# Branch B of a hybrid encoder: four query heads of a key group in one product, meta products behind wide value products, one output tile for two pairs

## The chip, the cores and the metric

The kernel runs on one core of a Trainium2 chip, in one launch. The metric is the device time of one execution in microseconds (us); the median of three runs before the change is 1885.11 us (1883.92 to 1886.2). Five engines run side by side on a core: TensorE (PE; its weight loads are shown as PEld), VectorE (DVE), ScalarE (ACT), GpSimd (POOL) and SyncE (SP), which issues nearly all DMAs here. TensorE writes into PSUM banks, from which ScalarE and VectorE copy results into SBUF.

## The reference

One layer of an encoder is applied to two request groups with shared weights: a prompt of 2048 tokens and a sample of 512, each with 16 meta tokens in front, model width 1024. All is in float32. After a norm, one input projection gives queries, keys, values and gates for two attention branches, whose outputs are projected, gated, merged and projected again. Branch A is attention over a token grid. Branch B, which this case is about, is windowed attention with 8 query heads and 2 key and value heads of width 64, so each key group serves four query heads:

```python
s_band = jnp.einsum('bnqkgd,bnckd->bnkgqc', qr, k_band).astype(f32) * scale + band_bias
s_band = jnp.where(visible[:, None, None], s_band, NEG_INF)
s_meta = jnp.einsum('bnqkgd,bmkd->bnkgqm', qr, km).astype(f32) * scale + meta_bias
p = jax.nn.softmax(jnp.concatenate([s_band, s_meta, sink_col], axis=-1), axis=-1).astype(v.dtype)
o_real = (jnp.einsum('bnkgqc,bnckd->bnqkgd', p[..., :C], v_band)
          + jnp.einsum('bnkgqm,bmkd->bnqkgd', p[..., C:C + N_META], vm))
```

A block of 128 queries sees its own block of keys and the ones before and behind it (three blocks, or two at the ends of a sequence), the 16 meta keys, and a sink logit that counts in the denominator alone.

## The kernel before

Tokens are cut into five windows of 512 (window 0 is the sample). The input projections come first, up to about 980 us. Then follows the attention with the output side of the layer filled in between. Numbers are kept as a high and a low part in a reduced float32 (F32R), so that a product of two such numbers is made of two or three matmuls: high by high, high by low, low by high.

**Units and their order.** `units` (L1508) lists for each window 32 units of branch A (`unit_a`, L1074) and 16 of branch B (`unit_b`, L1171). A unit of branch B is a key group `gh` (two), a query block `n` (four) and a pair of heads `i` (two): 128 queries by two heads. Each unit is a generator with stages: loads (L1181 to L1205), scores (L1207 to L1227), normalisation (L1228), transposes and eviction (L1232), products with the values (L1264). The main loop (L1563) advances the units in a software pipeline: in step i it runs the loads of unit i+4, the scores of i+2, the normalisation of i+1, some dense work, the transposes of unit i, dense work again, and the products of unit i-1 last. The dense work (`fill`, L1544) is the output side of the layer, in portions of six matmuls of 512 columns; a unit of branch B gets one portion in each of its two places, or a little less in window 0. The order on TensorE is as written; on VectorE, ScalarE, GpSimd and SP a scheduler orders instructions.

**A unit of branch B.** Per head, two matmuls (L1223, L1224) give the scores of 128 queries against 402 columns (16 meta keys, the sink, a pad column, three blocks of 128) or 274 (two blocks). VectorE adds the bias and finds the maximum (L1047), ScalarE takes the exponential with its sum (L1054). The two heads lie in one tile `prs`, the first with its meta columns last and the second with its meta columns first (L1212), so that the meta columns of both heads are neighbours; for this, key and bias tiles hold the meta columns a second time behind the blocks (L1191, L1204, L1215). VectorE normalises one head and ScalarE the other (L1229).

TensorE then transposes each key block of each head (L1243) and once the 32 meta columns of the two heads (L1246). ScalarE copies the high part into `ph_` (L1250), VectorE the low part into `pl_` (L1251). These two tiles have 14 places of 128 columns; units use the places from 0 and from 6 in turn. For the meta columns, three copies (L1260 to L1262) fill one of two tiles `pms`: high part, low part, and the high part again, 96 rows in all.

The products: for each key block, one of the high probabilities (256 columns, two heads) with the values' high and low part side by side (128 weight columns, L1267) and one of the low probabilities with the high part (64 weight columns, L1272). Before the last low one stand two products of 128 columns, one per head, of `pms` with `vms`, the meta values laid out for the three parts and 64 weight columns (L1270). The sum's upper half holds the low values' part; ScalarE copies it (L1274) and VectorE adds the halves into `y32` (L1277), 128 columns a head. After the last block, `y32` is multiplied by the gate (L1280) and split into high and low (`y_split`, L1067): multiplication and low part on GpSimd, the copy on ScalarE. For the very last group VectorE does GpSimd's part. Each `y32` is 512 columns of two heads; the tag has two buffers, which branch A uses too (L1110).

**What else is on the engines.** Portions of dense work bring weight casts (L207 on ScalarE, L208 on GpSimd), gate multiplications, squares and sums. In branch A, L1141 are the transposes, L1156 and L1158 the products, L1164 the sum. `dense_fin` (L1361) uses the transposes' PSUM banks for L170 and L185.

Of the kernel before, what the change touches and what calls it, by code (L numbers as in the profile page):

```python
# [17 lines left out]
P = 128  # L18
# [77 lines left out]
def encoder_block(ctx: ExitStack, tc: tile.TileContext, xT, x_end, w_in, w_pa, w_pb, w_o, norm_g, final_g,  # L96
# [945 lines left out]
    HALF = 416  # L1042
# [24 lines left out]
    def y_split(br, w, p, y32, eng=nc.gpsimd):  # L1067
        if p == 0:
            ys[br, w] = tuple(yp.tile([P, 4, WTOK], F32R, tag=f"y{br}{i}", name=f"y{br}{i}{w}") for i in range(2))
        yh, yl = ys[br, w]  # L1070
        nc.scalar.copy(yh[:, p, :], y32)
        eng.tensor_sub(yl[:, p, :], y32, f32(yh[:, p, :]))

    def unit_a(w, p, h, g, sh):  # L1074
# [34 lines left out]
        if g == 0 and h == 0:  # L1109
            sh["y"] = at.tile([P, WTOK], F32, tag="y32", name="y32")  # L1110
# [14 lines left out]
        pr = at.tile([P, 2 * HALF], F32, tag="pr", name="pr", bufs=3)[:, :WTOK]  # L1125
# [45 lines left out]
    def unit_b(w, gh, n, i, sh):  # L1171
# [12 lines left out]
        if n == 0 and i == 0:  # L1184
            q = sh["q"] = ld.tile([P, 2, 2, WTOK], F32R, tag="q", name="q")
            for j in range(2):
                move(q[:, j], qb_d[w, p + j].rearrange("(h d) i t -> (d i) h t", h=2))
            bt = sh["b"] = ld.tile([P, 2, 2, EXTRA + 3 * P + N_META], F32, tag="ba", name="bb")
            for j in range(2):
                move(bt[:, j, :, : EXTRA + 3 * P], bias_b[p + j])  # L1190
                move(bt[:, j, 0, EXTRA + 3 * P :], bias_b[p + j][:, 0, :N_META])  # L1191
        if n == 0 and first:
            bt0 = sh["b0", i] = ld.tile([P, 2, EXTRA + 2 * P + N_META], F32, tag="b0", name="bb0")
            move(bt0[:, :, : EXTRA + 2 * P], bias_b0[p])
            move(bt0[:, 0, EXTRA + 2 * P :], bias_b0[p][:, 0, :N_META])
# [3 lines left out]
        if i == 0:  # L1199
            kt = sh["k"] = ld.tile([P, 2, EXTRA + 3 * P + N_META], F32R, tag="kd", name="kbt")  # L1200
            move(kt[:, :, EXTRA : EXTRA + nbk * P],
                 kb_d[gs].rearrange("d j i t -> (d j) i t")[:, :, b0 : b0 + nbk * P])
            move(kt[:, :, :EXTRA], kbm_d[gs].rearrange("d j i t -> (d j) i t"))
            move(kt[:, :, ncol : ncol + N_META], kbm_d[gs].rearrange("d j i t -> (d j) i t")[:, :, :N_META])  # L1204
        kt, q, z = sh["k"], sh["q"][:, i], sh.get(("z", i))  # L1205
        yield
        if n == 0:  # L1207
            sh["y", i] = at.tile([P, WTOK], F32, tag="y32", name="y32")
        y32 = sh["y", i]
        bt = sh["b0", i] if first else sh["b"][:, i]  # L1210
        prs = at.tile([P, 2 * HALF], F32, tag="pr", name="prs", bufs=3)
        cols = slice(HALF - ncol, HALF), slice(HALF, HALF + ncol)  # L1212
        k0 = HALF - ncol + EXTRA - N_META, HALF + EXTRA
        if nbk == 2 and not first:
            nc.vector.tensor_copy(bt[:, 0, ncol : ncol + N_META], bt[:, 0, :N_META])  # L1215
        sm = sums_of()
        for h in range(2):
# [4 lines left out]
            ks = slice(N_META * (1 - h), N_META * (1 - h) + ncol)  # L1222
            nc.tensor.matmul(s[:, :ncol], q[:, h, qs], kt[:, 0, ks], start=True, stop=False)  # L1223
            nc.tensor.matmul(s[:, :ncol], q[:, h, qs], kt[:, 1, ks], start=False, stop=True)  # L1224
            nm = scores_max(s, ncol, bt[:, h, ks])
            exps(prs[:, cols[h]], s[:, :ncol], nm, sm[:, h : h + 1])
        yield  # L1227
        rd = inverse(sm)  # L1228
        for h in range(2):  # L1229
            normalise(prs[:, cols[h]], prs[:, cols[h]], rd[:, h : h + 1], on_act=h == 1)  # L1230
        yield
        slots = [("k", j) for j in range(nbk)] + [("m", 0)]  # L1232
        parts = []
        c0 = 6 * ((2 * n + i) % 2)
        for half in range(0, len(slots), 2):
            tp = ps_p.tile([P, WTOK], F32, tag="tp", name="tp")
            part = slots[half : half + 2]
            nk = sum(1 for t, _ in part if t == "k")
            for m, (t, j) in enumerate(part):
                c = 2 * m * P  # L1240
                if t == "k":
                    for h in range(2):
                        nc.tensor.transpose(tp[:, c + h * P : c + (h + 1) * P],  # L1243
                                            prs[:, k0[h] + j * P : k0[h] + (j + 1) * P], ident)
                else:
                    nc.tensor.transpose(tp[: 2 * N_META, c : c + P], prs[:, HALF - N_META : HALF + N_META], ident)  # L1246
            if nk:
                x = slice(c0 + 2 * half, c0 + 2 * half + 2 * nk)
                tb = tp[:, : nk * 2 * P].rearrange("p (b t) -> p b t", t=P)
                nc.scalar.copy(ph_[:, x], tb)  # L1250
                nc.vector.tensor_sub(pl_[:, x], tb, f32(ph_[:, x]))  # L1251
            for m, (t, j) in enumerate(part):
                c = slice(2 * m * P, 2 * (m + 1) * P)
                if t == "k":
                    x = slice(c0 + 2 * (half + m), c0 + 2 * (half + m) + 2)
                    parts.append((j, *(t[:, x].rearrange("p b t -> p (b t)") for t in (ph_, pl_))))
                else:
                    pm = pms[(2 * n + i) % 2]
                    tm = tp[:32, c.start : c.start + P]
                    nc.scalar.copy(pm[0:32], tm)  # L1260
                    nc.vector.tensor_sub(pm[32:64], tm, f32(pm[0:32]))
                    nc.scalar.copy(pm[64:96], f32(pm[0:32]))  # L1262
        yield
        o = ps_o.tile([P, WTOK], F32, tag="o", name="ob")  # L1264
        for m, (j, hi, lo) in enumerate(parts):
            vb = sh["v"][:, (b0 - tlo) // P + j, :]
            nc.tensor.matmul(o[:, : 2 * P], vb, hi, start=(m == 0), stop=False, skip_group_check=True)  # L1267
            if m == nbk - 1:
                for h in range(2):
                    nc.tensor.matmul(o[:64, h * P : (h + 1) * P], vms[:, gh, h, :], pms[(2 * n + i) % 2], start=False,  # L1270
                                     stop=False, skip_group_check=True)
            nc.tensor.matmul(o[:64, : 2 * P], vb[:, :64], lo, start=False, stop=m == nbk - 1, skip_group_check=True)  # L1272
        ol = at.tile([64, WTOK], F32, tag="ol", name="ol", bufs=1)[:, : 2 * P]
        nc.scalar.copy(ol, o[64:128, : 2 * P])  # L1274
        for h in range(2):
            hs = slice(64 * h, 64 * h + 64)
            nc.vector.tensor_add(y32[hs, qs], o[:64, h * P : (h + 1) * P], ol[:, h * P : (h + 1) * P])  # L1277
        if n == 3:
            eng = nc.vector if w == NWIN - 1 and gh else nc.gpsimd
            eng.tensor_mul(y32, y32, z)  # L1280
            y_split("b", w, p, y32, eng)
# [253 lines left out]
    pms = [yp.tile([96, P], F32R, tag=f"pms{i}", name=f"pms{i}") for i in range(2)]  # L1535
    vms = yp.tile([96, 2, 2, 64], F32R, tag="vms", name="vms")
# [3 lines left out]
    with tc.manual_schedule(engines={E.PE}):  # L1540
# [17 lines left out]
        vbm = vbm_d.rearrange("m g (h f) -> m g h f", h=2)  # L1558
        for h in range(2):
            for r, part in ((0, 0), (32, 0), (64, 1)):  # L1560
                move(vms[r + 16 * h : r + 16 * h + 16, :, h], vbm[:, :, part, :])
        next(units[0][2])
        for i in range(N):  # L1563
# [12 lines left out]
            fill(share)  # L1576
            next(units[i][2])
# [3 lines left out]
            if i:  # L1581
# [111 lines left out]
```

## Time and profile before

| | |
|---|---|
| median of 3 runs | 1885.11 us |
| the profiled execution | 1884.6 us, its span 1882.6 us |
| branch B's units | from 1072.5 us (first transposes) to 1802 us (last products), beside branch A's |
| 1390 to 1472 us, branch B of window 2: TensorE busy | 81.74 of 82 us |
| the same: ScalarE, VectorE, GpSimd | 71.62, 65.54, 43.38 us |

The span runs from the program's first instruction to its last in one profiled execution. A group line of the profile has line, engine, operation, tiles (out<-in), shape and count, then busy time and the mean of one in ns, then the engine's idle time before and what ended it. A line of the order of time has start, duration, engine, line, operation, tiles and shape, with "xN" for N merged instructions, and in brackets idle time before it. Matmuls are pipelined: a matmul's duration holds its latency, and the distance from one start to the next tells what it takes of TensorE's time.

### The profile page before, as it was taken

How to read it: one execution, taken by the hardware profiler on the slowest of the kernel's cores; microseconds unless marked ns; L12 is line 12 of the kernel's file. 1: busy time of each engine (PE TensorE's matmuls, PEld its weight loads, DVE VectorE, ACT ScalarE, POOL GpSimd, SP SyncE). 2: the span in 40 equal slices, each digit the busy share in tenths (PEclk: the TensorE clock that was granted, in tenths of full speed). 3: DMA queues.
4: the chain of work that ended last, by engine and by line, in shares of the span. 5: the costliest groups of instructions: out<-in, count | busy, mean ns of one | idle time of the engine just before them, and what ended most of it. 6: DMA issues, size and time to landing. Idle time of an engine off the chain costs nothing. (4 is left out here: it accounts for less than half of the span.)

```text
span 1882.6 us, 29816 instructions
## 1 busy us (share of the span) xinstructions
PE 1857.5 (99%) x9797; PEld 1585.1 (84%) x9797; DVE 1326.1 (70%) x2961; ACT 1144.5 (61%) x2528; POOL 729.2 (39%) x558
## 2 busy tenths in 40 slices
PE   8999999999999999999999999999999999999998
PEld 6988888888888888888888888888888888888887
DVE  8985667556477565544457888878887877888874
ACT  6444444434365444444456797797789778878932
POOL 2005343323203222322324435656744763685420
PEclk9999999999999999999999999999999999999999
DMA  7675666655295677644259878977986997697483
GB/s 262 199 195 183 194 184 182 209 188 179 84 341 185 189 216 199 208 139 160 104 187 316 274 221 265 305 213 249 319 275 187 316 307 227 218 315 259 118 301 133
DMA packets 288145, 414.35 MB, mean 220 GB/s; under 512 B 117736, under 2 KB 162360, under 8 KB 286456
## 3 DMA queue, kind: packets, MB, share of 16 engines
q1 hardware_dynamic: 287704, 412.45, 68.1%
q8 instruction: 78, 1.28, 0.3%
q14 instruction: 75, 0.61, 0.1%
q10 hardware_dynamic: 288, 0.01, 0.0%
HBM read 303.46 MB, written 108.91 MB: 219 GB/s over the span
## 5 line engine op out<-in xcount | busy, mean ns | idle before, releaser
L208 POOL TENSOR_TENSOR wt<-wraw,wt 128x512 fp32r<-128x512 f32 x164 | 213.0, 1317 | 266.9 <-ACT wt L207 266.8
L850 PE MATMUL pa<-u,wt 128*128 128x512 f32 x1008 | 244.5, 392 | 2.1 <-ACT wt L207 1.1
L850 PE MATMUL pa<-u,x 128*128 128x512 f32 x984 | 236.7, 389 | 0.4 <-ACT u L861 0.4
L850 PEld LDWEIGHTS pa<-u,wt 128*128 128x128 f32 x1008 | 189.9, 189 | 42.4 <-ACT wt L207 1.5
L207 ACT CAST wt<-wraw 128x512 fp32r<-128x512 f32 x312 | 178.0, 619 | 74.8 <-PE mm L148 29.8
L850 PEld LDWEIGHTS pa<-u,x 128*128 128x128 f32 x984 | 184.5, 188 | 39.2 <-ACT u L861 0.8
L821 POOL TENSOR_TENSOR s<-wraw,raw 128x512 f32<-128x512 f32 x40 | 58.2, 1456 | 279.4 <-DVE x L208 279.4
L146 PE MATMUL mm<-u,wt 128*128 128x512 f32 (+2 forms) x416 | 150.4, 362 | 7.1 <-ACT u L334 7.1
L816 POOL TENSOR_TENSOR s<-raw 128x512 f32<-128x512 f32 x40 | 58.1, 1454 | 232.8 <-DMA raw<-in_w_in_dram 116.0
L147 PE MATMUL mm<-u,wt 128*128 128x512 f32 (+2 forms) x416 | 146.8, 353 | 1.1 <-DVE u L335 1.1
L148 PE MATMUL mm<-u,wt 128*128 128x512 f32 (+2 forms) x416 | 146.6, 352 | 0.0
L208 DVE TENSOR_TENSOR wt<-wraw,wt 128x512 fp32r<-128x512 f32 x148 | 104.5, 744 | 52.3 <-ACT wt L207 52.1
L850 PE MATMUL pe<-u,wt 128*128 128x512 f32 x504 | 121.4, 390 | 0.0
L850 PE MATMUL pc<-u,wt 128*128 128x512 f32 x504 | 121.1, 389 | 0.0
L850 PE MATMUL pe<-u,x 128*128 128x512 f32 x480 | 115.3, 389 | 0.0
L850 PEld LDWEIGHTS pe<-u,wt 128*128 128x128 f32 x504 | 94.6, 188 | 19.6
L850 PEld LDWEIGHTS pc<-u,wt 128*128 128x128 f32 x504 | 94.6, 188 | 19.6
L1145 DVE TENSOR_TENSOR pl<-tp,ph 128x384 fp32r<-128x384 f32 (+6 forms) x160 | 94.9, 593 | 20.9 <-ACT ph L1144 18.7
L1144 ACT CAST ph<-tp 128x384 fp32r<-128x384 f32 (+6 forms) x160 | 81.5, 510 | 43.0 <-PE tp L1141 41.4
L146 PE MATMUL pso<-mh,wt 128*128 128x512 f32 x256 | 107.1, 418 | 0.0
L829 POOL TENSOR_TENSOR s<-wraw,s 128x512 f32<-128x512 f32 x40 | 54.0, 1350 | 136.3 <-DVE wt L208 136.3
L850 PEld LDWEIGHTS pe<-u,x 128*128 128x128 f32 x480 | 90.1, 188 | 18.7
(258 smaller groups left out, 5024.8 us busy)
## 6 DMA issues: line engine op xcount, KB each, us to landing
wraw<-in_w_in_dram SPq DMA_DIRECT2D x86, 512.0 KB
raw<-in_w_in_dram SPq DMA_DIRECT2D x40, 512.0 KB
q<-qa SPq DMA_DIRECT2D x40, 512.0 KB
wraw<-in_w_o_dram SPq DMA_DIRECT2D x32, 512.0 KB
kbt<-kb SPq DMA_DIRECT2D x32, 384.0 KB
qa<-evq SPq DMA_DIRECT2D x20, 512.0 KB
qb<-evq SPq DMA_DIRECT2D x20, 512.0 KB
ka<-evk SPq DMA_DIRECT2D x20, 512.0 KB
```

The source lines that it names most:

```text
L146: nc.tensor.matmul(ps, wh, uh, start=first, stop=False)
L147: nc.tensor.matmul(ps, wh, ul, start=False, stop=False)
L148: nc.tensor.matmul(ps, wl, uh, start=False, stop=last)
L207: nc.scalar.copy(h, r)
L208: low[0] = (eng or lo_eng[0]).tensor_sub(l, r, f32(h)).ins
L816: eng.tensor_add(s1, a21, a22)
L821: eng.tensor_sub(s3, a11, a21)
L829: eng.tensor_sub(s4, a12, s2)
L850: nc.tensor.matmul(ps, wt[:, a, s], u[:, b, kk, :], start=first and kk == 0 and i == 0, stop=kk == 3 and i == 2, skip_group_check=True)
L1144: nc.scalar.copy(ph_[:kb, a], tb)
L1145: nc.vector.tensor_sub(pl_[:kb, a], tb, f32(ph_[:kb, a]))
```

## The change

The two units of a block (`i` = 0 and 1) now share what comes after the transposes, so that four heads go through the products together.

- `ph_` and `pl_` hold a key block as four places, one a head; the two units fill two each. The products of a pair run once, in the second unit's last stage: high and low of 512 columns per key block. The first unit's last stage is empty.
- GpSimd multiplies the meta columns of each unit by the inverse sums into a small tile `mt` (four heads of 16 columns). One transpose for the pair, behind the second unit's last key block, gives 64 rows; ScalarE copies the high part into rows 0 to 63 of `pms`, VectorE the low part into rows 64 to 127. There is one `pms`. `vms` has 128 weight columns per head, and four meta products a pair: one behind each high product, the rest behind the first low product.
- The copy of the sum's upper half is 512 wide, and two additions of 256 columns (two pairs of heads by 128) go into an output tile for two pairs, which has one buffer. Branch A's head pairs share this tile two by two as well.
- The meta columns stay first (in a window's first block of a sequence, last), with no second copy of them; normalisation covers the key blocks alone. The bias of a sequence's first block lies behind the other in one tile: the tile `b0`, the extra DMAs and the copy of L1215 go.
- In the main loop, products of unit i-1 come before the transposes of unit i wherever one of the two is of branch B.

```diff
@@ unit_a @@
         if g == 0 and h == 0:
-            sh["y"] = at.tile([P, WTOK], F32, tag="y32", name="y32")
+            if p % 2 == 0:
+                pair[0] = at.tile([P, 2, WTOK], F32, tag="y32", name="y32", bufs=1)
+            sh["y"] = pair[0][:, p % 2]
@@ unit_b @@
         for h in range(2):
-            normalise(prs[:, cols[h]], prs[:, cols[h]], rd[:, h : h + 1], on_act=h == 1)
+            normalise(prs[:, h, band], prs[:, h, band], rd[:, h : h + 1], on_act=h == 1)
+        nc.gpsimd.tensor_mul(mt[:, 2 * i : 2 * i + 2, :], prs[:, :, meta : meta + N_META],
+                             rd[:, :, None].broadcast_to([P, 2, N_META]))
         yield
...
+            end = i == 1 and j0 + 2 > nbk
+            if end:
+                tm = tp[: 4 * N_META, 2 * nk * P : (2 * nk + 1) * P]
+                nc.tensor.transpose(tm, mt.rearrange("p n m -> p (n m)"), ident)
             if nk:
-                x = slice(c0 + 2 * half, c0 + 2 * half + 2 * nk)
...
+                ph, pl = (t[:, 4 * j0 : 4 * (j0 + nk)].rearrange("p (j i h) t -> p j i h t", i=2, h=2)[:, :, i]
+                          for t in (ph_, pl_))
+                tb = tp[:, : nk * 2 * P].rearrange("p (j h t) -> p j h t", h=2, t=P)
+                nc.scalar.copy(ph, tb)
+                nc.vector.tensor_sub(pl, tb, f32(ph))
+            if end:
+                nc.scalar.copy(pms[:64], tm)
+                nc.vector.tensor_sub(pms[64:], tm, f32(pms[:64]))
+        yield
+        if i == 0:
+            yield
+            return
         o = ps_o.tile([P, WTOK], F32, tag="o", name="ob")
-        for m, (j, hi, lo) in enumerate(parts):
+        for j in range(nbk):
             vb = sh["v"][:, (b0 - tlo) // P + j, :]
-            nc.tensor.matmul(o[:, : 2 * P], vb, hi, start=(m == 0), stop=False, skip_group_check=True)
-            if m == nbk - 1:
-                for h in range(2):
-                    nc.tensor.matmul(o[:64, h * P : (h + 1) * P], vms[:, gh, h, :], pms[(2 * n + i) % 2], start=False,
+            hi, lo = (t[:, 4 * j : 4 * j + 4].rearrange("p b t -> p (b t)") for t in (ph_, pl_))
+            for y, (out, vals, src) in enumerate(((o, vb, hi), (o[:64], vb[:, :64], lo))):
+                nc.tensor.matmul(out, vals, src, start=j + y == 0, stop=j + y == nbk, skip_group_check=True)
+                for m in (range(nbk, 4) if j == 0 else ()) if y else (j,):
+                    nc.tensor.matmul(o[:, m * P : (m + 1) * P], vms[:, gh, m, :], pms, start=False,
                                      stop=False, skip_group_check=True)
-            nc.tensor.matmul(o[:64, : 2 * P], vb[:, :64], lo, start=False, stop=m == nbk - 1, skip_group_check=True)
-        ol = at.tile([64, WTOK], F32, tag="ol", name="ol", bufs=1)[:, : 2 * P]
-        nc.scalar.copy(ol, o[64:128, : 2 * P])
+        ol = at.tile([64, WTOK], F32, tag="ol", name="ol", bufs=1)
+        nc.scalar.copy(ol, o[64:128])
+        ov, lv = (t.rearrange("p (i h t) -> p i h t", i=2, h=2) for t in (o[:64], ol))
         for h in range(2):
-            hs = slice(64 * h, 64 * h + 64)
-            nc.vector.tensor_add(y32[hs, qs], o[:64, h * P : (h + 1) * P], ol[:, h * P : (h + 1) * P])
+            nc.vector.tensor_add(sh["y"][64 * h : 64 * h + 64, :, qs], ov[:, :, h], lv[:, :, h])
         if n == 3:
             eng = nc.vector if w == NWIN - 1 and gh else nc.gpsimd
-            eng.tensor_mul(y32, y32, z)
-            y_split("b", w, p, y32, eng)
+            for j in range(2):
+                y32 = sh["y"][:, j]
+                eng.tensor_mul(y32, y32, sh["z", j])
+                y_split("b", w, p - 1 + j, y32, eng)
@@ main loop @@
             fill(share)
+            early = i and "b" in (br, units[i - 1][0])
+            if early:
+                next(units[i - 1][2])
             next(units[i][2])
...
             fill(share)
-            if i:
+            if i and not early:
                 next(units[i - 1][2])
```

More of the change, by code (lines that the diff above doesn't have):

```diff
@@ L1040, in encoder_block @@
     ys = {}
-    HALF = 416
+    HALF = EXTRA + 3 * P
     def scores_max(s, n, bias):
@@ L1072, in y_split @@
         eng.tensor_sub(yl[:, p, :], y32, f32(yh[:, p, :]))
+    pair = [None]
     def unit_a(w, p, h, g, sh):
@@ L1231, in unit_b @@
         yield
[L1232 to L1235, printed above, removed]
+        for j0 in range(0, nbk + i, 2):
             tp = ps_p.tile([P, WTOK], F32, tag="tp", name="tp")
[L1237 to L1241, printed above, removed]
-                    for h in range(2):
[L1243 to L1246, printed above, removed]
-            if nk:
-                x = slice(c0 + 2 * half, c0 + 2 * half + 2 * nk)
[L1249 to L1262, printed above, removed]
@@ L1557, in encoder_block @@
             pass
[L1558 to L1561, printed above, removed]
+        for m in range(4):
+            move(vms[N_META * m : N_META * (m + 1), :, m, :], vbm_d)
+            move(vms[64 + N_META * m : 64 + N_META * (m + 1), :, m, :64], vbm_d[:, :, :64])
         next(units[0][2])
```

54 lines of the change are left out of this document (27 added, 27 removed).

## The prediction

> **What bounds the kernel now.** I read the page's engine sums first, then the sums of a stretch inside one branch B phase, then the groups by shape, then TensorE's order of time in branch B, and last what waits there.
>
> ```profile
> span 1882.6 us, 29816 instructions
> ...
> PE 1857.5 (99%) x9797; PEld 1585.1 (84%) x9797; DVE 1326.1 (70%) x2961; ACT 1144.5 (61%) x2528; POOL 729.2 (39%) x558
> ```
>
> ```profile
> 1395.00:1435.00 40.00, 40.00 (x246) 35.65 (x245) 30.75 (x89) 36.08 (x94) 18.10 (x15) 1.00 0.62 187
> ```
>
> The second fence is a stretch of a branch B phase (columns: TensorE, weight loads, VectorE, ScalarE, GpSimd, granted clock, DMA). TensorE is busy for all 40.00 us at full granted clock; ScalarE follows with 36.08. So an edit is worth what it takes from TensorE's stream, less any wait it brings; ScalarE and VectorE matter only by how late they hand TensorE its operands. The waits view shows almost nothing to recover:
>
> ```profile
> PE fin_v L170 <- DVE pms L1261: 0.5, 2, 0.3
> PE ob L1267 <- DVE y L1277: 0.5, 1, 0.5
> ```
>
> **The counts.** Rows picked from the groups by shape; columns: count | busy us, mean ns | idle before:
>
> ```profile
> L1246 PE MATMUL tp<-ident,prs 128*32 128x128 f32 x80 | 21.8, 273 | 0.0
> L1267 PE MATMUL ob<-ph,vb 128*128 128x256 f32 x224 | 56.4, 280 | 0.5 <-DVE y L1277 0.5
> L1272 PE MATMUL ob<-pl,vb 128*64 128x256 f32 x224 | 60.0, 282 | 0.0
> L1270 PE MATMUL ob<-pms,vms 96*64 96x128 f32 x160 | 22.7, 223 | 0.0
> L1223 PE MATMUL s<-kbt,q 128*128 128x402 f32 x128 | 44.6, 349 | 0.0
> ```
>
> There are 80 units, two heads each (80 meta transposes). Two units share a block, so 40 pairs; a pair has four of the score products of L1223, and 128 of them have 402 columns (three key blocks), so 128/4 = 32 pairs have three blocks and the other 8 have two. The means are latencies and overlap, so I price by the distance from start to start:
>
> ```profile
> 1240.19 0.28 PE L1267 MATMUL ob<-ph,vb 128*128 128x256 f32 x1
> 1240.19 0.13 PEld L1272 LDWEIGHTS ob<-pl,vb 128*64 128x64 f32 x1
> ...
> 1240.78 0.28 PE L1270 MATMUL ob<-pms,vms 96*64 96x128 f32 x2
> 1240.90 0.29 PE L1272 MATMUL ob<-pl,vb 128*64 128x256 f32 x1
> 1241.02 0.34 PE L1223 MATMUL s<-kbt,q 128*128 128x402 f32 x1
> ...
> 1243.13 0.82 PE L1243 MATMUL tp<-ident,prs 128*128 128x128 f32 x6
> 1243.78 0.27 PE L1246 MATMUL tp<-ident,prs 128*32 128x128 f32 x1
> 1243.81 0.48 PE L146 MATMUL pso<-mh,wt 128*128 128x512 f32 x1
> 1244.12 0.40 PE L147 MATMUL pso<-ml,wt 128*128 128x512 f32 x1
> ...
> 1245.27 0.28 PE L1267 MATMUL ob<-ph,vb 128*128 128x256 f32 x1
> ```
>
> - Five value products of 256 columns take 1240.19 to 1240.78: 0.118 us each.
> - Two meta products of 128 columns take 0.12: 0.060 each.
> - Five dense products of 512 columns run from 1244.12 to 1245.27: 0.230 each.
> - Six transposes take 0.65: 0.108 each. The meta transpose costs as much: from its start to L147 pass 0.34 us, of which one dense product is 0.230.
>
> **Meta transposes.** One for four heads instead of one for two: 40 fewer, 40 x 0.108 = 4.3 us off TensorE.
>
> **Value products.** 448 of 256 columns become 224 of 512: 448 x 0.118 = 52.9 against 224 x 0.230 = 51.5, so 1.4 us off. The streamed columns are the same; only a few ns of each start are saved.
>
> **Meta products.** Still 160 of 128 columns, 9.6 us before and after. But their weights double from 64 to 128 columns:
>
> ```profile
> L1270 PEld LDWEIGHTS ob<-pms,vms 96*64 96x64 f32 x160 | 20.3, 136 | 0.0
> L1267 PEld LDWEIGHTS ob<-ph,vb 128*128 128x128 f32 x224 | 42.1, 188 | 4.6 <-issue 0.9 <-ACT prs L1054 0.6
> ```
>
> Behind a product of 512 columns (0.230) such a load hides, and the 64-column load of the low product hides beneath the meta product, as it does today. What is not covered is a 128-column load beneath a 128-column product. With three blocks it comes once a pair (the fourth meta product, then the next high product), with two blocks twice (two meta products in a row, then a high one): 32 + 16 = 48 places. No row of this kernel shows that very sequence. From below it is 0 (all hidden); from above the whole load shows, 0.188 - 0.060 = 0.128, so 6.1 us. I take the transposes' 0.108 as nearest, since each of them also loads 128 columns behind 128 streamed: 48 x (0.108 - 0.060) = 2.3 us added. [...]
>
> TensorE's stream: -4.3 - 1.4 + 2.3 = **-3.4 us**, bounds -5.7 and +0.4.
>
> **ScalarE, VectorE, GpSimd: beside the stream.**
>
> ```profile
> L1274 ACT COPY ol<-ob 64x256 f32<-64x256 f32 x80 | 29.5, 369 | 6.4 <-PE ob L1272 4.6
> L1262 ACT CAST pms<-pms 32x128 fp32r<-32x128 f32 x80 | 23.7, 297 | 2.1
> L1260 ACT CAST pms<-tp 32x128 fp32r<-32x128 f32 x80 | 20.2, 253 | 12.1 <-DVE pl L1251 11.4
> L1280 POOL TENSOR_TENSOR y<-y,z 128x512 f32<-128x512 f32 x18 | 23.1, 1286 | 23.1 <-DVE y L1277 18.7 <-DMA wraw<-in_w_pa_dram 4.4
> ```
>
> Per pair ScalarE loses two L1260 and two L1262 (1.10 us) for one cast of about 0.25, and two copies (0.74) for one twice as wide, which costs between 0.37 and 0.74: about 1 us less in a pair's 10 us, so near 80% busy instead of 90%. VectorE has two adds of twice the width for four, and one meta subtraction less. All of that is hidden now beneath TensorE, so it is worth nothing by itself; it makes operands earlier. GpSimd gets 80 small multiplies (32 columns). No row shows one; from below near nothing, from above 1.29 us (L1280); I take 0.3. GpSimd is busy 18.10 of 40 us, and the multiply is ready at least a unit (5 us) before its transpose. If that cover fails, the second unit's transposes wait for it. The dropped DMAs (16-column key and bias pieces, the separate first-block bias) leave SP's queue shorter, which no wait of TensorE in branch B asks for.
>
> **One output tile.** Two pairs of heads share one buffer, so the first sum of the next group waits until GpSimd and ScalarE have finished with the last: four GpSimd steps of 1.29 and two casts, some 6 us of work, against two units, about 10 us, until that sum. If other GpSimd work eats the margin, VectorE waits at the add, and behind it queue evictions and score maxima; TensorE feels it only past the 2 to 4 us that these lead it. In branch A the margin is four units. I take 0.
>
> **The products move ahead of the next transposes.** The split probabilities of a pair now have one place, so its products go before the next unit's transposes. Today an evicted set has one more unit to get ready. For the second unit of a pair the time left is the distance to the next transposes, less the products that stand between today (1240.19 to 1241.02, 0.83). Three second units of one phase, each with its transposes, its meta subtraction and the next unit's transposes, picked from the order of time:
>
> ```profile
> 1425.16 0.81 PE L1243 MATMUL tp<-ident,prs 128*128 128x128 f32 x6
> 1429.04 0.28 DVE L1261 TENSOR_TENSOR pms<-tp,pms 32x128 fp32r<-32x128 f32 x1 [0.32 <-ACT pms L1260]
> 1430.22 0.82 PE L1243 MATMUL tp<-ident,prs 128*128 128x128 f32 x6
> 1435.32 0.82 PE L1243 MATMUL tp<-ident,prs 128*128 128x128 f32 x6
> 1440.41 0.81 PE L1243 MATMUL tp<-ident,prs 128*128 128x128 f32 x6
> 1441.32 0.28 DVE L1261 TENSOR_TENSOR pms<-tp,pms 32x128 fp32r<-32x128 f32 x1
> ...
> 1457.04 0.81 PE L1243 MATMUL tp<-ident,prs 128*128 128x128 f32 x6
> 1460.33 0.28 DVE L1261 TENSOR_TENSOR pms<-tp,pms 32x128 fp32r<-32x128 f32 x1 [0.32 <-ACT pms L1260]
> 1462.64 0.82 PE L1243 MATMUL tp<-ident,prs 128*128 128x128 f32 x6
> ```
>
> First: 5.06 - 0.83 = 4.23 to the products, 4.46 to the first meta product (it stands behind a wide one); ready after 4.16. Second: 4.49 allowed, ready after 6.28, so 1.8 late. Third: 5.60 - 0.83 + 0.23 = 5.00 allowed, ready after 3.57. So two of three fit with today's latencies. The late one is late because nothing urged it: VectorE and ScalarE put other work between. With 1 us less in ScalarE's queue per pair, and no output copy or sums between these transposes and their products, I take no wait there, with bounds of 0 and 1.8 x 40 = 72 us. Today's two waits of fin_v for pms and the one for y (1.0 us together) belong to handovers that become fewer; I count half: -0.5.
>
> **Sum.** -3.4 - 0.5 = -3.9 us. The profiled execution took 1884.6 us (span 1882.6 and 2.0 around it), 0.5 below the median of 1885.11. So 1880.7 for it, and **1881.2 us** for the median. A measurement of this kernel can tell about 0.2% (3.8 us) from no change; the forecast lies at that edge.
>
> **Rivals.**
>
> *The late meta operand (slower).* The place is the first meta product of each pair: if VectorE and ScalarE keep today's latencies, the three units above give 1.8/3 = 0.6 us a pair, 24 us over 40, and with the stream's -3.4 the kernel takes about 1906. From 0.08 us a pair the gain is gone, from 0.18 it is slower beyond 0.2%. For it: ScalarE's 36.08 of 40 us, and all slack of a unit removed. Against: two of three fit, and the queues get shorter. Chance 0.14.
>
> *The same wait, small.* At 0.1 us a pair it takes 4 us: 1885. Chance 0.20.
>
> *The stream does better.* If the fourth meta product's load hides after all, the stream gives -5.7, and with the 1.0 us of present waits gone the kernel takes 1878.4. For it: a load starts together with the product before it (L1272's at 1240.19, with L1267). Against: six transposes at 0.108. Chance 0.17.
>
> *Loads in series.* If a load ran only after the product before it, the change would save 112 loads of 0.188 and 112 of 64 columns (0.136, as L1270's), 36 us, and add 160 x 0.052 = 8 for the wider meta weights: about 1857. Against it: 0.118 between products whose loads last 0.188. [...] Chance 0.02.
>
> **Chances.** The forecast has 0.47, by itself 1879 to 1883.5, of which 0.26 lies beyond 0.2% and 0.21 within. Faster: 0.26 + 0.17 + 0.02 = 0.45. Same: 0.21 + 0.20 = 0.41. Slower: 0.14. The range 1876.5 to 1889.5 takes in the better stream with its bounds and the late operand up to 0.2 us a pair; about 0.17 stays outside, mostly above.
>
> **What would show it.** After the change: 224 value products at 0.230 from start to start; 40 meta transposes; meta products at 0.060 behind wide ones and near 0.108 where two narrow ones follow; TensorE still full in the middle of branch B; ScalarE near 80% there. Wrong would be an idle time of the meta or low products with ScalarE or VectorE as the releaser, transposes waiting for GpSimd, or a VectorE that waits for GpSimd at the output sums while TensorE stands.

## The result and the profile after

| | before | after |
|---|---|---|
| median (lowest to highest), 6 runs each on one chip | 1884.64 us (1883.73 to 1886.2) | 1899.94 us (1897.94 to 1901.09) |
| ratio of the times | | 1.0079, 95% interval 1.0066 to 1.0092 |
| profiled execution, its span | 1884.6, 1882.6 us | 1897.9, 1896.1 us |

The change is 15.3 us slower where 3.9 us less was forecast. The page of the kernel after begins:

```profile
span 1896.1 us, 29007 instructions
...
PE 1859.7 (98%) x9533; PEld 1573.2 (83%) x9533; DVE 1314.4 (69%) x2833; ACT 1109.0 (58%) x2368; POOL 748.6 (39%) x638
```

There are 264 TensorE instructions fewer, all the other engines but GpSimd have less to do, and the span is 13.5 us longer. A stretch of branch B in window 2, 5 us later on the clock than the prediction's, shows no trouble at all:

```profile
1400.00:1440.00 40.00, 40.00 (x217) 34.48 (x217) 32.27 (x80) 33.12 (x81) 20.60 (x23) 1.00 0.58 187
```

TensorE is full, ScalarE fell from 36.08 to 33.12 of 40 us. The loss is elsewhere. The waits of TensorE from 970 us on, in the kernel after (engine, tile, line, releaser: us in total, times, longest):

```profile
PE ob L1265 <- DVE pms L1253: 13.1, 13, 3.2
PE s L1219 <- ACT prs L1054: 2.1, 4, 0.8
PE tp L1239 <- DVE pl L1250: 1.3, 1, 1.3
```

L1265 is a meta product, and L1253 is VectorE's half of the copy that makes its operand, the transposed meta probabilities `pms`. Before, the longest entry of this view was another:

```profile
PE tp L1141 <- DVE pr L1065: 2.9, 4, 1.9
```

So TensorE stands at the first meta product of a pair, where the slower rival had put it. The same view, cut to the branch B phases of the five windows, gives 3.2 us in 3 times in window 0, one wait of 0.9, 0.9 and 0.8 us in windows 1, 2 and 3, and in window 4 more than half:

```profile
PE ob L1265 <- DVE pms L1253: 7.2, 7, 3.2
```

**One balance.** For every TensorE instruction, from the first to the last of the program, I took the distance from its start to the next one's start, and summed these by what the first instruction does. Such sums leave nothing out between the two: their total differs between the two kernels by 13.8 us, as the span does (13.5).

| us | before | after | difference |
|---|---|---|---|
| branch B products (value and meta) | 62.7 | 82.4 | +19.7 |
| branch B transposes | 53.1 | 49.3 | -3.8 |
| branch B scores | 57.2 | 59.2 | +2.0 |
| branch A scores (and the waits behind them) | 58.6 | 55.3 | -3.3 |
| all else | 1635.9 | 1635.1 | -0.8 |

The products hold it. An undisturbed pair with three key blocks takes 1.69 us (32 of them), one with two blocks 1.28 (8): 64.3 us, or 1.6 more than before. The other 18.1 us are late operands and what follows from them. The waiting pairs are 15 of 40, and from the start of the first wide product to that of the meta product they lose 15.3 us.

**Why the operand is late.** First a pair in the middle of window 2 that just fits. Its transposes start at 1419.34. ScalarE's and VectorE's evictions, then the products:

```profile
1420.25 0.85 ACT L1249 CAST ph<-tp 128x512 fp32r<-128x512 f32 x2
1422.05 0.26 ACT L1252 CAST pms<-tp 64x128 fp32r<-64x128 f32 x1 [0.44 <-DVE pl L1250]
```

```profile
1421.01 1.01 DVE L1250 TENSOR_TENSOR pl<-tp,ph 128x512 fp32r<-128x512 f32 x2
1423.27 0.28 DVE L1253 TENSOR_TENSOR pms<-tp,pms 64x128 fp32r<-64x128 f32 x1
```

```profile
1423.62 0.40 PE L1263 MATMUL ob<-ph,vb 128*128 128x512 f32 x1
1423.85 0.22 PE L1265 MATMUL ob<-pms,vms 128*128 128x128 f32 x1
```

`pms` is ready at 1423.55 and wanted at 1423.85: 0.30 us to spare, and seven more pairs of windows 2 and 3 look the same to 0.02 us. It comes last of all the pair's operands, though the second matmul already needs it. And ScalarE's small copy L1252 starts when VectorE's last `pl` has ended (1422.02). The same wait stands 21 times among the 40 pairs; the group line gives 11.0 us of ScalarE's idle time to it:

```profile
L1252 ACT CAST pms<-tp 64x128 fp32r<-64x128 f32 x40 | 10.3, 257 | 11.1 <-DVE pl L1250 11.0
```

With three key blocks the meta transpose shares a PSUM tile with the last block's transposes, and the two engines read that tile in turn. So the chain is `ph`, `pl`, `pms`, `pms`: four steps in series, and each can be held by other work of its engine. At the handover from branch B to A there are only 2.64 us, from the transposes at 1303.74 to the first product at 1306.38. VectorE, then TensorE:

```profile
1304.99 1.02 DVE L1250 TENSOR_TENSOR pl<-tp,ph 128x512 fp32r<-128x512 f32 x2 [0.29 <-ACT ph L1249]
1306.58 0.70 DVE L1047 CUSTOM_DVE_ANT_0 s<-s,ba 128x512 f32<-128x512 f32 x1 [0.57 <-PE s L1122]
1307.20 0.14 DVE L1047 DVE_READ_ACCUMULATOR2_ANT nm<- 128x1 f32 x1
1307.37 0.28 DVE L1253 TENSOR_TENSOR pms<-tp,pms 64x128 fp32r<-64x128 f32 x1
```

```profile
1307.71 0.33 PE L1265 MATMUL ob<-pms,vms 128*128 128x128 f32 x1 [0.93 <-DVE pms L1253]
```

ScalarE's half was done at 1306.31, but VectorE's queue has the score maximum of branch A ahead of `pms`; it waits 0.57 us for that score and then works 0.70 on it. The worst pair is in window 4: transposes at 1771.85, ScalarE's copy only at 1778.15, behind seven instructions of other work that ScalarE has taken up since 1775.36, VectorE's at 1779.38, and TensorE stands 3.20 us.

### The profile page after: what moved, and what is told of

Same layout as the page of the kernel before. It is cut to its first block, busy times and chain, and to the rows that moved or that the text cites. A ratio compares the mean times of both kernels' runs of the same rounds, so it can differ in the third digit from the quotient of the medians.

```text
span 1896.1 us, 29007 instructions
## 1 busy us (share of the span) xinstructions
PE 1859.7 (98%) x9533; PEld 1573.2 (83%) x9533; DVE 1314.4 (69%) x2833; ACT 1109.0 (58%) x2368; POOL 748.6 (39%) x638
## 4 chain that ended last, share of the span: by engine, by line
PE 87%; DVE 5%; ACT 3%; DMA 2%; issue 1%; SPq 1%; POOL 0%; DVEq 0%; ACTq 0%
PE pa L850 23%; PE pe L850 12%; PE pc L850 6%; PE tp L1145 3%; PE pso L148 3%; PE pso L146 3%; PE pso L147 3%; PE ob L1263 3%; PE mm L148 3%; PE mm L146 3%; PE mm L147 2%; PE tp L1239 2%; PE psb L148 2%; PE psb L146 2%; PE psb L147 2%; PE psa L146 2%
## 5 line engine op out<-in xcount | busy, mean ns | idle before, releaser
L1054 ACT ACTIVATE prs<-s,nm 128x402 f32<-128x402 f32 (+1 forms) x160 | 91.1, 574 | 54.8 <-DVE nm L1047 44.5
L1047 DVE CUSTOM_DVE_ANT_0 s<-s,ba 128x384 f32<-128x384 f32 (+5 forms) x160 | 86.9, 544 | 31.2 <-PE s L1122 28.4
```

Of the source, the lines that this page charges most:

```text
L1047: nc.vector.tensor_tensor_reduce(s[:, :n], s[:, :n], bias, -1.0, 3.0e38, ALU.add, ALU.min, nm)
L1054: nc.scalar.activation(out, s, AF.Exp, bias=nm, scale=-1.0, accum_out=sm)
```

## The experiments

Theory L: the first meta product of a pair is a deadline that the change brought forward and that the last of four serial evictions misses. Rivals: the evicting engines are short of time in general, so that any order makes something late; the turn-taking on the PSUM tile; VectorE standing at the output sums; branch A. All kernels were timed against the kernel before on the same chip.

**Meta copy first** (the changed kernel, the two `pms` instructions ahead of the wide copies):

```
             if end:
+                nc.scalar.copy(pms[:64], tm)
+                nc.vector.tensor_sub(pms[64:], tm, f32(pms[:64]))
...
-            if end:
-                nc.scalar.copy(pms[:64], tm)
-                nc.vector.tensor_sub(pms[64:], tm, f32(pms[:64]))
```

> The changed kernel, with the copies of the meta columns (ScalarE's high part, VectorE's low part) written ahead of those of the key blocks of the same transposes. Theory L (the late meta operand): the first meta product waits for these two copies in 15 of 40 pairs, 15.3 us in all, only because they stand behind both evictions of the key blocks; put first, they are ready near 2.5 us after the first transpose where 2.9 to 4.5 are allowed, the waits fall below 2 us, the half clock after the longest wait goes too, and the time falls by 14 to 19 us, to 1881 to 1886. Rival Q (all evictions are too late since the products moved ahead of the next transposes): the key blocks are delayed by what the meta columns gain, the wait moves to the high and low products, and the time stays within 3 us of the changed kernel, 1897 to 1903.

Measured: 1890.91 us, ratio 1.0028 (1.0016 to 1.0039). Two instructions moved by a few lines give back 9 of the 15 us. The waits of TensorE:

```profile
PE tp L1145 <- DVE pr L1065: 3.3, 3, 1.9
PE s L1219 <- ACT prs L1054: 2.2, 4, 0.7
PE ob L1265 <- DVE pms L1247: 1.7, 3, 0.9
PE tp L1239 <- DVE pl L1253: 1.2, 1, 1.2
PE ob L1263 <- DVE pl L1253: 1.0, 2, 0.7
...
PE ob L1263 <- ACT ph L1252: 0.6, 1, 0.6
```

The wait for `pms` fell from 13.1 to 1.7, as L says, but small waits on the wide copies (0.6 and 1.0) and branch A's waits (3.3) came in. It ended between L's range and the rival's, nearer to L. The group line of the second wide copy shows where the turn-taking went: now that one waits for VectorE's `pms`.

```profile
L1252 ACT CAST ph<-tp 128x256 fp32r<-128x256 f32 x64 | 23.9, 373 | 12.8 <-DVE pms L1247 12.8
```

**The order alone** (the kernel before, with each unit's products ahead of the next unit's transposes, and nothing else of the change):

```
             fill(share)
+            early = i and "b" in (br, units[i - 1][0])
+            if early:
+                next(units[i - 1][2])
             next(units[i][2])
...
-            if i:
+            if i and not early:
```

> The kernel before, with one part of the change alone: products of unit i-1 ahead of the transposes of unit i wherever one of the two is of branch B. Theory L: the order alone makes the wait. Today the third copy of the meta columns ends between 2.2 and 7.6 us after a unit's first transpose, and the first meta product would stand about 4.7 us after it (fewer in window 0 and at handovers); so TensorE waits at L1270 for ScalarE, by 0.2 to 0.6 us a unit over 80 units, and the time is 1900 to 1930. Rival T (the order costs nothing by itself; the wait comes with the pair's single transpose, GpSimd's multiply and the single pms): within 3 us of the kernel before, 1882 to 1888.

Measured: 1935.23 us, ratio 1.0267 (1.025 to 1.0284): 50 us slower, worse than L's range.

```profile
PE ob L1270 <- ACT pms L1262: 22.8, 18, 2.4
PE ob L1270 <- DVE pms L1261: 12.0, 14, 1.1
```

The order is the harmful part. The rest of the change together takes back 35 us of what it costs; which part of the rest does it (one meta set for two units, ScalarE's shorter queue) is not shown.

**Meta products late** (the changed kernel; each pair's meta products behind its last four value products instead of behind each from the first):

```
+            wide += [(o, vb, hi), (o[:64], vb[:, :64], lo)]
+        before = len(wide) - 4
+        for y, (out, vals, src) in enumerate(wide):
+            nc.tensor.matmul(out, vals, src, start=y == 0, stop=False, skip_group_check=True)
+            if y >= before:
+                m = y - before
+                nc.tensor.matmul(o[:, m * P : (m + 1) * P], vms[:, gh, m, :], pms, ...)
```

> The changed kernel, with the four meta products of a pair behind the last four wide products in place of the first ones. Theory L: with three key blocks the first meta product stands 0.46 us later (two wide products more ahead of it), with two blocks nothing changes; the 15 waits lose 0.46 us each where there are three blocks, 15.3 us become about 10.6, so 1894 to 1896. Rival Q (the wide products' own operands are late too, behind the meta ones): the wait stays as long, 1898 to 1902, and is seen at a high or low product.

Measured: 1895.5 us, ratio 1.0059 (1.0041 to 1.0076), as L expected. With three blocks the deadline moves by two wide products, 0.46 us, and the wait falls accordingly:

```profile
PE ob L1269 <- DVE pms L1253: 7.9, 12, 2.8
```

**More time at the handover** (the changed kernel; where a branch A unit follows, both portions of dense work go ahead of the last pair's products):

```
+                if br == "a":
+                    fill(share)
...
-            fill(share)
+            if not (early and br == "a"):
+                fill(share)
```

> The changed kernel, but in the step in which branch B hands over to branch A both portions of dense work come ahead of the last products, not one before and one behind. Theory L: at the handovers out of windows 0 to 3 only 2.3 to 2.6 us lie between the transposes and the products, and the waits there are 0.05, 1.10, 1.09 and 0.99 us, 3.2 in all; with the second portion ahead they vanish, 3 us less, 1896 to 1898. Rival R (these waits only take up slack that the next branch A window gives back, since its loads bind): no change, 1899 to 1901.

Measured: 1904.47 us, ratio 1.0101 (1.0084 to 1.0118), slower than both expected. The handovers' waits did go, and another came:

```profile
PE ob L1265 <- DVE pms L1253: 10.4, 10, 3.2
PE tp L1145 <- DVE pr L1065: 6.7, 5, 2.1
```

Those are branch A's transposes. Behind them is VectorE, which stands at a gate tile whose load has not landed. VectorE's waits for these loads from 1320 to 1570 us, in the kernel before and in this one:

```profile
DVE sgb L1332 <- DMA sgb<-gb: 7.9, 4, 2.9
```

```profile
DVE sgb L1328 <- DMA sgb<-gb: 7.6, 3, 3.1
```

In the changed kernel the same entry is 2.3 us. So the kernel before has this stall, the changed kernel loses most of it (the -3.3 us of branch A's scores in the balance; why is not shown), and variants get it back.

**The meta transpose in a tile of its own**, with the meta copy first:

```
-                tm = tp[: 4 * N_META, 2 * nk * P : (2 * nk + 1) * P]
+                tm = ps_p.tile([P, WTOK], F32, tag="tp", name="tm")[: 4 * N_META, :P]
```

> The meta transpose gets a PSUM tile of its own (so a bank of its own) and is still evicted first; nothing else differs from the variant that evicted it first out of the shared bank (1890.9 us). Theory B (the two engines that evict take turns on one bank, so that putting the meta copy first only moved the lateness to the wide copies): TensorE's waits on the wide copies in branch B, 1.6 us in that variant, fall under 0.5, its waits on the meta copy stay under 2, and the kernel takes 1887 to 1890. Rival F (the bank does not matter, the rest is branch A's waits and the loads): 1890 to 1892. Rival T (a third PSUM tile for each pair is missing elsewhere: transposes wait for a free tile): 1893 or more, with transposes of branch B waiting for VectorE's subtractions.

Measured: 1906.4 us (1899.18 to 1910.98), ratio 1.0106 (1.0074 to 1.0137). Rival T: three such tiles are used in turn, a pair with three blocks now takes five of them for four, and transposes wait for a free one.

```profile
PE tm L1244 <- DVE pl L1253: 4.9, 6, 1.3
PE fin_v L170 <- DVE pl L1253: 3.1, 2, 1.5
```

The second wide copy, idle for 12.8 us with the shared tile, hardly waits any more, so the shared tile does make the engines take turns:

```profile
L1252 ACT CAST ph<-tp 128x256 fp32r<-128x256 f32 x64 | 24.3, 380 | 0.3 <-PE tp L1239 0.2
```

What this is worth by itself stays open, since the cure costs more. Besides the waits, the mean granted clock of the profiled execution was 0.995 (span 1903.9 us), where the kernel with the meta copy first in the shared tile had 0.999 (1889.9); what is missing to 1 is 9.5 us of the one span and 1.9 of the other, so some 6 to 9 us more, an estimate from the rounded clocks.

**First and late together**, in the shared tile and with a tile of its own (the edits above, combined):

> Meta copy evicted first and, besides, the meta products placed last in each pair, behind wide products (both edits helped alone: 1890.9 and 1895.5 against 1899.9). Theory L (the first meta product is the deadline that is missed): the two act on the same wait, so they do not add up; TensorE's wait on the meta copy is under 0.7 us, waits on the wide copies stay near 1.6, and the kernel takes 1887 to 1890. Rival S (the evicting engines are simply short of time and any order makes some operand late): the waits on the wide copies grow to 4 us or more and the time stays at 1890 to 1895.

> The meta transpose in a PSUM tile of its own, evicted first, and the meta products last. Theory L with B: hardly a wait of TensorE in branch B is left (under 1 us in all), and what stays over the sum of the instructions is branch A's: 1884 to 1888. Rival S: 1889 or more, with waits on the wide copies.

Measured: 1891.59 us, ratio 1.0032 (1.0019 to 1.0046), and 1900.75, ratio 1.0083 (1.0063 to 1.0103). Placing the meta products late adds nothing once the copy is first. The first kernel's time lies 1.6 us above L's range and in rival S's, but its waits are not those of S: the products wait 1.2 us for `ph` and 1.0 for `pl`, 2.2 where S wanted 4 or more and L 1.6, and 1.8 for `pms`, where L wanted under 0.7. Branch A's stall (1.8 us) is in it besides, which led to the next experiment. The second kernel misses L's range by 12.8 us: there the meta transposes again wait 3.2 us for a free tile and the sums of `fin_v`, which use the same tiles, 3.1. Its time is in S's range, but no wait on the wide copies is in its list.

**Four gate tiles** (meta copy first, meta products late, and in the two places that allocate gate tiles):

```
-        t = pools["d"].tile([P, WTOK], F32, tag="sg", name=name, bufs=3)
+        t = pools["d"].tile([P, WTOK], F32, tag="sg", name=name, bufs=4)
```

> Meta copy first and meta products last, and one more buffer (four for three) for the gate tiles that the dense work loads. Theory G (branch A's waits on VectorE's normalised scores come from VectorE standing at a gate tile whose load was issued late because its buffer was still in use): VectorE's wait for the gate loads falls from about 7 us to under 2, TensorE's waits in branch A from about 3 to under 1, and the kernel takes 2 to 4 us less than the same kernel with three buffers: 1884 to 1887. Rival H (the load is late for the queue or the transfer, not for the buffer): the same time within 1 us as with three buffers.

Measured: 1889.17 us, ratio 1.0018 (1.0008 to 1.0028), 2.4 less than with three. Theory G's difference came true, though not its end value.

```profile
PE s L1219 <- ACT prs L1054: 2.2, 4, 0.7
PE tp L1239 <- DVE pl L1253: 1.9, 1, 1.9
PE ob L1269 <- DVE pms L1247: 1.7, 3, 0.9
```

Branch A's transposes are gone from the list, and so is VectorE's wait for these loads between 1320 and 1570 us. This is the best version with the change's order, and it is not faster than the kernel before. The kernel before was not run with four gate tiles, so how much it would gain by them is open.

**The output step later.** VectorE's waits in the kernel after have a new longest entry, at the output sums:

```profile
DVE y L1271 <- ACT ol L1268: 40.9, 34, 3.8
```

Before it was 3.0 us (L1277). A step that stands 40 us in front of evictions is a suspect. First it was moved in the program, behind the next unit's transposes (a `yield` ahead of the output copy, and one more call per unit):

> The changed kernel, with one step moved in program order: the output copy and the output sums of a pair come after the next unit's transposes and evictions (as they did before the change), not between the products and these transposes. TensorE's order is the same to the instruction. Theory D (because the products moved ahead of the next transposes, the output step moved ahead of their evictions too; VectorE stands 40.9 us there for ScalarE's copy, and this makes the next copies late): VectorE's wait for the output copy falls under 10 us, TensorE's wait for the meta copy from 13.1 to under 8, and the kernel takes 1890 to 1896. Rival N (this idle time of VectorE lies where it has nothing urgent, and the meta copy is late by its place behind the wide copies): 1898 to 1902, with the wait for the meta copy at 11 to 15. Rival O (with one PSUM bank for the output sum, the later copy keeps the next products waiting): waits of the first value product on VectorE's sums, 1902 or more.

> The kernel with the meta copy first, the meta products last and four gate tiles (1889.2), and with the output step moved behind the next unit's evictions as well. Theory D: the waits on the wide copies that are left there (1.9, 1.2 and 1.0 us) and the one on the meta copy (1.7) fall under 2.5 in all, and the kernel takes 1883 to 1887. Rival N: 1888 to 1890.

Measured: 1899.51 us and 1889.14, the times of the kernels they started from (1899.94 and 1889.17). They prove nothing: the instructions of VectorE, ScalarE and GpSimd came out in the same order to the last one, since the scheduler (the expectations call it the planner) and not the program orders them. Both are repetitions, and show that a kernel's median comes back within half a microsecond. Then VectorE's sums were tied to its queue behind the next unit's last subtraction:

```
+                evicted[0] = nc.vector.tensor_sub(pl, tb, f32(ph)).ins
...
+        with tc.issue_after(evicted[0]):
             for h in range(2):
                 nc.vector.tensor_add(sh["y"][64 * h : 64 * h + 64, :, qs], ov[:, :, h], lv[:, :, h])
```

> The move of the output step in the program left every engine's order as it was, since VectorE, ScalarE and GpSimd are ordered by the planner; so it was a repetition of the changed kernel (1899.5) and tested nothing. Here VectorE's two output sums are tied behind VectorE's last subtraction of the next unit's transposes. Theory D (VectorE standing for the output copy, 40 us in all, is what makes the meta copy late): its wait for the copy falls under 10 us, TensorE's wait for the meta copy from 13.1 to under 8, and the kernel takes 1890 to 1896. Rival N (VectorE stands there at times when it has nothing urgent, and the lateness comes from the meta copy's place behind the wide copies and from what stands between): 1897 to 1902 and a wait of 11 to 15 us. Rival O (sums that come later keep the single output bank busy, or push score maxima back): above 1902.

> The kernel with the meta copy first, the meta products last and four gate tiles (1889.2, and 1889.1 in its repetition), with the output sums tied behind the next unit's subtractions. Theory D: the waits on the wide and meta copies that are left, 5.9 us in all, fall under 3, and the kernel takes 1883 to 1887. Rival N: 1888 to 1891. Rival O: above 1891.

Measured: 1908.43 us, ratio 1.0122 (1.0105 to 1.0139), and 1893.42, ratio 1.0039 (1.0024 to 1.0054): 8.5 and 4.3 us slower than without the tie. The first one's waits:

```profile
PE ob L1267 <- DVE pms L1254: 15.0, 14, 2.3
```

```profile
DVE pl L1251 <- ACT ph L1250: 41.6, 28, 3.9
```

The sums themselves now wait 1.3 us, VectorE stands as long at another instruction, and TensorE waits 15.0 us for `pms` where it was 13.1. In the second kernel TensorE's waits on the copies (3.8 for `pms`, 1.3 and 1.1 for `pl`, 0.8 for `ph`) are 7.0 us in all, where they were 5.8. So theory D falls. That VectorE's 40 us at the sums did no harm at all is not shown, since the tie brings waits of its own. Both times lie in rival O's ranges, but its mechanism is not seen either: no product waits for VectorE's sums.

## Why the prediction was wrong

The failed step is the one that begins "The products move ahead of the next transposes", with its result "I take no wait there": it took three units of one phase for all 40 pairs. In its place the runs showed 18.1 us of waits for `pms` and what follows from them. The terms of TensorE's stream held, and two that the sum did not have came in at the scores:

| term of the sum | predicted | measured |
|---|---|---|
| 40 meta transposes less | -4.3 us | -4.4 (six transposes 0.573 from start to start, seven 0.682); the balance has -3.8, with waits such as the 1.3 us for `pl` in it |
| value products and the meta products' wider loads | -1.4 + 2.3 = +0.9 | +1.6 (64.3 for 62.7) |
| waits for `pms` and what follows from them | 0 | +18.1 |
| branch B scores | 0 | +2.0, of which 1.5 are waits for `prs` (2.1 for 0.6) |
| present waits that go | -0.5 | about -1, none of the three is in the list after |
| branch A scores | 0 | -3.3, nothing that the prediction had in mind (above) |

**The stream.** The products of a three-block pair, in the order of time of the kernel after:

```profile
1413.49 0.40 PE L1263 MATMUL ob<-ph,vb 128*128 128x512 f32 x1
1413.72 0.22 PE L1265 MATMUL ob<-pms,vms 128*128 128x128 f32 x1
1413.79 0.39 PE L1263 MATMUL ob<-pl,vb 128*64 128x512 f32 x1
1414.02 0.22 PE L1265 MATMUL ob<-pms,vms 128*128 128x128 f32 x1
1414.08 0.44 PE L1263 MATMUL ob<-ph,vb 128*128 128x512 f32 x1
1414.36 0.22 PE L1265 MATMUL ob<-pms,vms 128*128 128x128 f32 x1
...
1415.17 0.82 PE L1239 MATMUL tp<-ident,prs 128*128 128x128 f32 x6
```

A wide product takes 0.23, a meta product 0.06 to 0.07, and the one load that nothing wide covers shows at 1414.08: 0.28 to the next start instead of 0.23. That is the 0.05 that was priced from the transposes (0.048).

**The copies beside the stream.** They went as forecast: ScalarE at 33.12 of 40 us (83%, "near 80%"), GpSimd's multiply at 0.291 us for 0.3, no wait of TensorE for it, and none of VectorE for the shared output tile. No run with a second output tile tests that directly.

**The wait.** The three sampled units all came from the middle of one phase, window 2, and there the answer was right: the pairs that take their places in the kernel after (transposes at 1429.48, 1439.60 and 1460.80) are in time by 0.30, 0.14 and 0.17 us. Even the argument for the late unit held: its `pms`, ready 6.28 us after its first transpose before, is ready after 4.37. What failed was to take this sample for all pairs. The same working, done in the trace of the kernel before for every second unit that has a next one (39 of 40), finds 19 of them late, by 18.2 us in all: 9.4 in window 4, 4.2 in window 0, and 0.8, 1.8 and 1.9 in windows 1, 2 and 3. Of the 15.3 us that the pairs then lost, 8.4 lie in window 4, 3.7 in window 0, and 1.0 to 1.2 in each of the others, at the handover but for 0.05. At the handover shown 2.64 us are left where the sample had 4.23 and more; in windows 0 and 4 ScalarE and VectorE, behind other work, come to `pms` after up to 5.7 and 7.8 us (in window 4, too, a unit's portion of dense work is a little smaller, 30 for 32 by `COUNT`); and the meta copy was left the last of four steps in series.

The slower rival, at a chance of 0.14, had the place and the mechanism. That its size was near, 24 us against 18.1, is luck: the 24 stood on the sample's one late unit, and the pair in its place lost nothing.

What the runs add to this: the lateness is mostly one of order and not of load. With the same instructions, a few lines apart, the wait for `pms` goes from 13.1 to 1.7 us and the time from 1899.9 to 1890.9; pushing the deadline instead gives 1895.5. What is left in the best version against the kernel before, 4.6 us in the profiled spans, is by the same balance (4.7 in all) +6.9 in the products (1.6 of it the stream), +2.3 in the scores, -2.2 in the transposes, -3.5 in branch A's scores, and +1.3 for all else.

## What to carry to other kernels

When an edit shortens the time between the making of an operand and its use, work out that time at every kind of place (first phase, handover, last phase) and not only in the steady middle, and let the operand that is wanted first be made first. A sample from one phase says nothing of the others: here the trace of the kernel before, read over all pairs, already held nearly the whole loss and its main places. Before an idle engine is called the cause, move the instruction at which it idles, and look whether the built order really changed and what new waits the move brings.

## What the runs showed of the hardware

**The granted clock after stalls.** After the 3.20 us stall in window 4 TensorE's granted clock was 0.54 over 3.70 us. Two stretches of the kernel after, the stall and what follows (columns as in the prediction, the granted clock last but two):

```profile
1776.30:1779.70 3.40, 0.22 (x1) 0.00 (x0) 1.50 (x5) 2.73 (x8) 3.14 (x4) 1.00 0.57 150
1779.72:1783.42 3.70, 3.70 (x16) 3.13 (x16) 0.00 (x0) 0.58 (x1) 0.00 (x0) 0.54 0.21 74
```

The next stretch, 1783.42 to 1786.00, is back at 1.00. At 0.54 of the clock 3.70 us do the work of about 2.0, so some 1.7 us are lost beyond the stall's 3.2, an estimate. In the version with four gate tiles the clock fell behind two shorter stalls, 1.17 and 0.74 us within 2.5 us:

```profile
1771.00:1773.00 2.00, 0.83 (x6) 0.57 (x5) 0.33 (x2) 2.00 (x7) 2.00 (x3) 1.00 0.26 45
1773.00:1774.48 1.48, 0.74 (x4) 0.44 (x5) 1.08 (x2) 0.38 (x1) 0.85 (x2) 1.00 0.76 293
1774.48:1775.34 0.86, 0.86 (x8) 0.86 (x7) 0.00 (x0) 0.62 (x2) 0.00 (x0) 0.67 0.55 121
1775.34:1778.05 2.71, 2.71 (x9) 2.13 (x7) 1.86 (x4) 0.82 (x2) 0.00 (x0) 0.50 0.15 58
```

TensorE was busy 1.57 of 3.48 us, and then had 0.67 of the clock for 0.86 us and 0.50 for 2.71, with work waiting; from 1778.05 to 1780.00 it had 0.97. The length of the stalls does not settle it here. In the kernel before, two of 1.07 and 1.00 us in the input projections, the second ending at 130.82, were followed by half the clock, and one of 1.87 us, ending at 1525.49, by the whole:

```profile
131.32:134.73 3.41, 3.41 (x10) 2.64 (x9) 3.41 (x7) 1.36 (x3) 0.00 (x0) 0.50 0.34 135
1525.49:1529.00 3.51, 3.51 (x23) 3.17 (x24) 2.40 (x8) 3.28 (x9) 2.71 (x4) 1.00 1.01 316
```

In the kernel after, the same two stalls of the input projections, 1.07 and 1.01 us, the second ending at 131.80, were not followed by it:

```profile
131.80:135.20 3.40, 3.40 (x15) 2.82 (x16) 3.40 (x6) 2.65 (x6) 0.00 (x0) 1.00 0.35 140
```

No run was made to find what does.
